# Hybrid decoder layer on one core: the residual scaled at the front, sums of squares inside the out-projection, and all top-k look-ups on VectorE

## The chip, the cores and the metric

One core of a Trainium2 chip runs the whole layer in one launch. The metric is device time in microseconds (us), the median of several executions. The engines are TensorE (PE, with its weight loads as PEld), VectorE (DVE), ScalarE (ACT), GpSimd (POOL) and SyncE (SP, which only issues transfers here). Each runs its own instructions in order; semaphores tie them together.

## The reference, cut to what matters

All arrays are float32. D is 1024, there are 1024 positions and 16 learned tokens in front of them that are dropped at the end.

```python
h = layer_norm(concat([meta, x]), ln_emb_g, ln_emb_b)
q, k, v, xr, gr = split(h @ w_in)                     # 5 x 512 columns
attn = stick_breaking_attention(q, k, v)              # 8 heads of 64
lru  = rg_lru(causal_conv(xr)) * gelu(gr)
mixed = concat([rms_norm(attn, attn_norm_g), rms_norm(lru, lru_norm_g)]) @ w_out
h = layer_norm(DEEPNORM_ALPHA * h + mixed, ln1_g, ln1_b)

# PEER: for each of 8 heads, the 16 best of 128 x 128 experts by two half keys
s1, s2 = q1 @ sub_keys[0].T, q2 @ sub_keys[1].T       # 128 scores each
v1, i1 = top_k(s1, 16);  v2, i2 = top_k(s2, 16)
sc, sel = top_k(all sums v1 + v2, 16)
idx = take(i1 * 128 + i2, sel)                        # the look-up
w = softmax(sc) * gelu(down[idx] . h)
h = layer_norm(DEEPNORM_ALPHA * h + sum(w * up[idx]), ln2_g, ln2_b)
```

## The kernel before, in words

Positions are worked in eight blocks of 128. The program is one straight list of instructions; a planner sorts each engine's list at build time by readiness and priority (earlier source lines first), and instructions issued through the handle `W` instead of `V` keep their order. A tile's memory is reused once every reader of the old tile is done, and `bufs` says how many copies a name has.

**Front (the loop over `LNB`, L278 to L302).** Nine `xt` tiles are loaded, normalised by ACT in place (L281), stored to the scratch array `xh_d` from the POOL queue (L283), transposed by PE, and split into a high and a low part `hT` (DVE, L297 and L300). Every product in the kernel is three matmuls of such parts (`mm3`, L127 to L129). The tiles of the recurrent unit, `y` first, then take over the memory of the front's pools `ga` and `lw`.

**Recurrent unit and attention (to L607).** The last of four pairs of heads (p == 3) also holds the recurrent half of the out-projection. `lru_load(j)` loads a block `hr` back from `xh_d` and POOL multiplies it by `eg` and adds `eb` (L556, L557), the embedding norm's scale and shift times ALPHA. `lru_mix` adds the projected part into `hr` on DVE (L567) and stores it to `ah_d`. On the attention path DVE does a scan (L481) and a product (L482) for each unit, PE transposes the result, and DVE or ACT copies the transposes (`aT`, L505 and L507) for the product with the values (`po`, L513).

**Out-projection (`mix_out`).** `prep(j+1)` runs one block ahead of `body(j)`: it loads the attention output into `ml`, squares it (`sq`, one buffer, L548), splits it in place into `mh` and `ml`, sums the squares on PE (`ss`, L633) and forms `rra`, the inverse root (L635). `body(j)` multiplies two halves of 512 columns and adds each, times `rra`, to the block (L645). `tail(j-1)` transposes the block before for the next stage.

**Queries and top-k (`queries`).** For each of 8 heads PE makes queries and scores, and one or two "run-ahead" products (`run_ahead`) in between; all their weights are split by DVE (`dl`, L124). DVE picks the 16 best (`topk1`, `topk_pos`). `topk_look` then builds a one-hot tile `oh` on DVE (L740) and reduces it on an engine that is passed to it:

```python
W.tensor_tensor(oh, ab.., iotb, op=is_equal)            # L740, DVE
G.tensor_tensor(oh, oh, ib.., op=mult)                  # L741
G.tensor_tensor(oh[.. 0:8], oh[.. 0:8], oh[.. 8:16])    # L742, then L743, L744: halves again
G.tensor_tensor(selo[half], oh[.., 0], oh[.., 1])       # L745
```

For heads 0 to 6 that engine is POOL, for head 7 it is DVE. From head 2 on, `hyb(1)` calls between the picks handle block 5 of the positions row by row: POOL issues an indirect gather of an expert's row (`row`, L894; at most five in flight) and DVE takes its dot product with the block (L113, `row<-row,acc`) or adds it (L922).

**Gate matrices (the loop at L1000 on).** DVE (`bt` L1016, `ae` L1021), ACT and PE build the dense gates, with more `hyb` and run-ahead work in between, and `topk_x` does the same top-k for the last two blocks with pinned instructions; its look-up is on POOL too, with one `oh` buffer (`OHX = 1`).

**Main loop.** All experts' products for five blocks on PE, and gathered rows for the other blocks on DVE.

Of the kernel before, what the change touches and what calls it, by code (L numbers as in the profile page):

```python
# [8 lines left out]
F32 = mybir.dt.float32  # L9
# [4 lines left out]
AF = mybir.ActivationFunctionType  # L14
ALU = mybir.AluOpType
# [4 lines left out]
P = 128  # L20
# [5 lines left out]
NT = S // P  # L26
NB = NT + 1
AW = 512
H = 8
# [3 lines left out]
EPS = 1e-5  # L33
# [4 lines left out]
ST = 2  # L38
# [21 lines left out]
OHX = 1  # L60
# [16 lines left out]
def layer_kernel(ctx, tc, x, meta, vecs, chan, lnc, w_in, gate_w, w_out, wq, skT, down, downT, up, out, dbg=None):  # L77
# [111 lines left out]
    with ExitStack() as c1:  # L189
# [53 lines left out]
        with ExitStack() as c2:  # L243
            ga = c2.enter_context(tc.tile_pool(name="ga", bufs=1, reuse_waits="tile"))
            lw = c2.enter_context(tc.tile_pool(name="lw", bufs=3, reuse_waits="tile"))
            tps = c2.enter_context(tc.tile_pool(name="tps", bufs=4, space=PSUM, reuse_waits="tile"))
            mv9 = ga.tile([P, NT + 1, 2], F32, name="mv9")
            ve9 = ga.tile([P, NT + 1], F32, name="ve9")
            rs9 = ga.tile([P, NT + 1], F32, name="rs9")
            nm9 = ga.tile([P, NT + 1], F32, name="nm9")  # L250
            V.memset(mv9, 1.0)
            xts = []
            for j in range(NT + 1):
                n = NM if j == 0 else P
                xt = lw.tile([P, D], F32, name="xt", bufs=NT + 1)
                SY.dma_start(xt[:n], meta if j == 0 else x[(j - 1) * P:j * P, :])
                xts.append(xt)
            convs = {i: conv_in(i) for i in range(XE)}

            def stats(j):  # L260
                n = NM if j == 0 else P
                st = small.tile([P, 2, 6], F32, name="lnst", tag="lnst")
                for i in range(2):
                    W.bn_stats(st[:n, i, :], xts[j][:n, i * 512:(i + 1) * 512])
                W.bn_aggr(mv9[:n, j], st[:n])

            for j in range(LNB[0][1]):
                stats(j)
            for bi, (j0, j1) in enumerate(LNB):
                js = slice(j0, j1)  # L270
                W.tensor_scalar(ve9[:, js], mv9[:, js, 1], EPS, None, op0=ALU.add)
                rsqrt_small(rs9[:, js], ve9[:, js], P, j1 - j0, f"ln{bi}", ga, W, (lambda: stats(j1)) if bi < 2 else None)
                W.scalar_tensor_tensor(nm9[:, js], mv9[:, js, 0], -1.0, rs9[:, js], op0=ALU.mult, op1=ALU.mult)
                if bi < 2:
                    for j in range(j1 + 1, LNB[bi + 1][1]):
                        stats(j)
            prep_slab()
            for j0, j1 in LNB:  # L278
                for j in range(j0, j1):
                    n = NM if j == 0 else P  # L280
                    A.activation(xts[j][:n], xts[j][:n], AF.Identity, bias=nm9[:n, j:j + 1], scale=rs9[:n, j:j + 1])  # L281
                    if j > 0:
                        G.dma_start(xh_d[(j - 1) * P:j * P, :], xts[j])  # L283
                c0 = 0 if j0 == 0 else NM + (j0 - 1) * P
                w = NM + (j1 - 1) * P - c0
                for c in range(KC):
                    pt = tps.tile([P, 512], F32, name="tr")
                    o = 0
                    for j in range(j0, j1):
                        n = NM if j == 0 else P  # L290
                        transpose(pt[:, o:o + n], xts[j][:n, c * P:(c + 1) * P])
                        o += n
                    tm = lw.tile([P, 3 * P], F32, name="tm")
                    A.activation(tm[:, :w], pt[:, :w], AF.Identity, bias=lc[:, 1, c:c + 1], scale=lc[:, 0, c:c + 1])
                    hi, lo = hT[0][:, c, c0:c0 + w], hT[1][:, c, c0:c0 + w]
                    if c % 2:
                        V.tensor_copy(hi, tm[:, :w])  # L297
                    else:
                        A.activation(hi, tm[:, :w], AF.Copy)
                    V.tensor_tensor(lo, tm[:, :w], hi.bitcast(F32), op=ALU.subtract)  # L300
                for xr, gen in convs.values():
                    next(gen)  # L302

        with ExitStack() as c2:
            vt = ap.tile([P, NB, AW], F32, name="vt")
# [246 lines left out]
            def lru_load(j):  # L552
                mh, ml = mixed(4, j)
                hr = wr.tile([P, D], F32, name="raw")
                SY.dma_start(hr, xh_d[j * P:(j + 1) * P, :])
                G.tensor_tensor(hr, hr, eg, op=ALU.mult)  # L556
                G.tensor_tensor(hr, hr, eb, op=ALU.add)  # L557
                return mh, ml, hr

            def lru_mix(j, mh, ml, hr):  # L560
# [13 lines left out]
            for p in range(4):  # L574
                cur = res.pop()
                gen = pair(p + 1, res) if p < 3 else iter(())
                for j in range(NT):
                    u = (p, j, *cur)
                    bes = att_a(u)
                    if prev is not None:  # L580
                        att_b(*prev)
                    prev = (u, bes)
                    next(gen, None)
                    if p == 2 and j == 6:
                        hctx.close()
                        wr = mixc.enter_context(tc.tile_pool(name="wr", bufs=2, side="right", reuse_waits="tile"))
                        wo = mixc.enter_context(tc.tile_pool(name="wo", bufs=2, side="right", reuse_waits="tile"))
                        mp = mixc.enter_context(tc.tile_pool(name="mp", bufs=1, side="right", reuse_waits="tile"))
                        mpa = mpx.enter_context(tc.tile_pool(name="mpa", bufs=1, side="right", reuse_waits="tile"))
                        eg = load_vec(mp, 0, "eg")  # L590
                        eb = load_vec(mp, 1, "eb")
                        A.activation(eg, eg, AF.Copy, scale=ALPHA)
                        A.activation(eb, eb, AF.Copy, scale=ALPHA)
                    if p == 2 and j >= 6:
                        for c in (4, 5) if j == 6 else (6, 7):
                            load_wo(c, wr, mpa)
                    if p == 2 and j == 7:
                        lnext = lru_load(0)
                    if p == 3:
                        lcur = lnext  # L600
                        if j + 1 < NT:
                            lnext = lru_load(j + 1)
                        lru_mix(j, *lcur)
                        if 2 <= j < 6:
                            load_wo(j - 2, wr, mp)
# [13 lines left out]
    def mix_out(h1, hTd, hTs):  # L619
        with mixc as c1:  # L620
# [5 lines left out]
            def prep(j):  # L626
                mh, ml, sq = first if j == 0 else mixed(0, j)
                SY.dma_start(h1[j], ah_d[j * P:(j + 1) * P, :])
                mv = wm.tile([P, 1], F32, name="mva")
                rra = wm.tile([P, 1], F32, name="rra")  # L630
                ss = sps.tile([P, 1], F32, name="ss")
                for c in range(4):
                    PE.matmul(ss, sq[:, c], ones, start=(c == 0), stop=(c == 3))  # L633
                V.tensor_scalar(mv, ss, 1.0 / AW, EPS, op0=ALU.mult, op1=ALU.add)
                rsqrt_small(rra, mv, P, 1, "ra", wm)  # L635
                return mh, ml, rra

            def body(j, mh, ml, rra):
                for hf in range(2):
                    cs = slice(hf * 512, hf * 512 + 512)  # L640
                    ps = zps.tile([P, 512], F32, name="z")
                    for c in range(4):
                        wh, wl = wch[c]
                        mm3(ps, mh[:, c], ml[:, c], wh[:, cs], wl[:, cs], c == 0, c == 3)
                    V.scalar_tensor_tensor(h1[j][:, cs], ps, rra, h1[j][:, cs], op0=ALU.mult, op1=ALU.add)  # L645
                layer_norm(h1[j], h1[j], P, None, None, None, None)

# [99 lines left out]
    def queries(hTd, hTs, zps, sps, pool, tkw, iotb, tv, sel):  # L747
# [3 lines left out]
        def second(h, vv, ii):  # L751
            cand = topk_cand(tkw, DT, vv)
            yield
            ab = topk_pos(V, tkw, DT, cand, tv[:, h])
            yield
            hs = slice(h * TOPK, (h + 1) * TOPK)
            topk_look(V, tkw, iotb, DT, ab, ii, [sel[:, half, :, hs] for half in range(2)], V if h == H - 1 else G, 2)
            yield

        def step():  # L760
# [181 lines left out]
    with ExitStack() as c1:  # L942
# [12 lines left out]
        def topk_x(h):  # L955
# [15 lines left out]
            ab = topk_pos(W, tkxw, ST, cand, tvx[:, h])  # L971
            yield
            hs = slice(h * TOPK, (h + 1) * TOPK)
            topk_look(W, tkxw, iotx, ST, ab, ii, [selx[:, half, :, hs] for half in range(2)], G, OHX)
            yield

        def index_x(h):
# [267 lines left out]
```

## Time and profile before

| | |
|---|---|
| median of 3 runs | 2960.87 us (2960.4 to 2962.03) |
| the profiled execution, its own time | 2963.82 us |
| its span in the profile | 2962.0 us, 44399 instructions |
| PE busy | 2783.2 us (94%) |
| PEld busy | 2492.6 us (84%) |
| DVE busy | 2487.0 us (84%) |
| ACT busy | 1148.1 us (39%) |
| POOL busy | 1453.4 us (49%) |
| mean granted PE clock | 0.973 |

Busy time is the time in which an engine has at least one instruction in work. Instructions of one engine overlap a little at their ends, so a sum of durations is slightly above the busy time. A granted clock of 1.00 is TensorE's upper level (2.4 GHz), 0.5 its lower (1.2 GHz); a mean in between says for what part of the stretch it was lowered.

### The profile page before, as it was taken

The page shows a single profiled execution, that of the slowest core. Times are in us where ns is not written, and L with a number is a line of the kernel's source. Part 1 is how long each engine was busy: PE and PEld are TensorE (multiplying, and loading weights), DVE is VectorE, ACT ScalarE, POOL GpSimd, SP SyncE. Part 2 cuts the span into 40 slices and gives each one's busy share as a digit, 9 for nine tenths or more (in the row PEclk, how much of TensorE's full clock was granted, in tenths as well). Part 3 has the DMA queues.
Part 4 walks back from the last instruction along what each step waited for, and adds up shares of the span by engine and source line. Part 5 has one row for each costly group of instructions (what it writes and reads, how often), then busy time and mean ns, then how long its engine had stood idle before and what let it go on. Part 6 is the DMA issues. An engine that isn't in the chain of part 4 may idle for free.

```text
span 2962.0 us, 44399 instructions
## 1 busy us (share of the span) xinstructions
PE 2783.2 (94%) x16311; PEld 2492.6 (84%) x16311; DVE 2487.0 (84%) x4610; ACT 1148.1 (39%) x2245; POOL 1453.4 (49%) x1202
## 2 busy tenths in 40 slices
PE   7999988889879989899989999999999999999997
PEld 6997766679879988889888888888888888888886
DVE  6246667768999999998769999999999999899997
ACT  6445553452212239787752223222222232222222
POOL 0003223343676655645435555556555666665653
PEclk9999988899989999999999999999999999999999
DMA  5123143413656668888789999999999999999992
GB/s 175 30 79 72 39 99 125 149 52 109 218 182 231 229 222 275 276 272 265 236 286 343 353 351 345 347 357 350 335 356 359 349 340 353 350 346 352 334 325 79
DMA packets 353946, 736.32 MB, mean 249 GB/s; under 512 B 26032, under 2 KB 164272, under 8 KB 353728
## 3 DMA queue, kind: packets, MB, share of 16 engines
q0 software_dynamic: 114304, 415.35, 39.5%
q1 hardware_dynamic: 234816, 316.03, 31.7%
q8 instruction: 128, 2.10, 0.3%
q10 hardware_dynamic: 4608, 2.10, 0.2%
q14 instruction: 90, 0.74, 0.1%
HBM read 645.24 MB, written 79.69 MB: 245 GB/s over the span
## 4 chain that ended last, share of the span: by engine, by line
PE 34%; DVE 23%; issue 17%; POOL 12%; DMA 11%; ACT 3%; SPq 0%; POOLq 0%; DVEq 0%; ACTq 0%
POOL row L894 9%; DMA row<-up,idx 6%; DVE row L113 4%; PE pp L127 3%; PE dps L127 3%; PE pp L128 3%; PE dps L129 3%; PE dps L128 3%; PE pp L129 3%; DVE dl L124 2%; DMA row<-down,idx 2%; PE g L1026 2%; PE po L513 2%; DVE h1s L1082 2%; PE z L127 2%
## 5 line engine op out<-in xcount | busy, mean ns | idle before, releaser
L127 PE MATMUL dps<-hTd,dl 128*128 128x320 f32 x2048 | 651.2, 318 | 47.0 <-DVE dl L124 40.7
L129 PE MATMUL dps<-hTd,dh 128*128 128x320 f32 x2048 | 646.6, 316 | 2.0 <-DVE hTd L124 2.0
L128 PE MATMUL dps<-hTd,dh 128*128 128x320 f32 x2048 | 647.3, 316 | 0.0
L894 POOL DMA_INDIRECT row<-down,idx x256 | 357.6, 1397 | 226.5 <-DVE act L113 188.8
L894 POOL DMA_INDIRECT row<-up,idx x256 | 343.6, 1342 | 233.9 <-DVE h1s L1082 196.3
L127 PEld LDWEIGHTS dps<-hTd,dl 128*128 128x128 f32 x2048 | 391.2, 191 | 53.0 <-DVE dl L124 32.9
L127 PE MATMUL ups<-uh,wl 128*128 128x512 f32 x1024 | 406.9, 397 | 2.6 <-DVE wl L124 2.0
L128 PE MATMUL ups<-uh,wh 128*128 128x512 f32 x1024 | 406.9, 397 | 0.0
L129 PE MATMUL ups<-ul,wh 128*128 128x512 f32 x1024 | 406.2, 397 | 0.5 <-DVE ul L124 0.5
L128 PEld LDWEIGHTS dps<-hTd,dh 128*128 128x128 f32 x2048 | 391.5, 191 | 3.0
L129 PEld LDWEIGHTS dps<-hTd,dh 128*128 128x128 f32 x2048 | 390.7, 191 | 2.3 <-DVE hTd L124 2.3
L1082 DVE SCALAR_TENSOR_TENSOR h1s<-row,gws,h1s 128x1024 f32<-128x1024 f32 x256 | 328.2, 1282 | 29.6 <-DMA row<-up,idx 27.5
L113 DVE CUSTOM_DVE_ANT_0 row<-row,h1s 128x1024 f32<-128x1024 f32 x256 | 307.1, 1221 | 36.8 <-DMA row<-down,idx 34.3
L123 ACT ACTIVATE wh<-gl 128x640 fp32r<-128x640 f32 x128 | 101.3, 792 | 606.4 <-DVE gl L1138 344.6
L894 POOL DMA_INDIRECT row<-up,idh x128 | 185.4, 1448 | 233.3 <-DVE acc L1072 84.4
L124 DVE TENSOR_TENSOR dl<-raw,dh 128x1024 fp32r<-128x1024 f32 x144 | 192.5, 1338 | 64.3 <-ACT dh L123 57.7
L129 PEld LDWEIGHTS ups<-ul,wh 128*128 128x128 f32 x1024 | 193.3, 189 | 48.3 <-DVE ul L124 1.0
L127 PEld LDWEIGHTS ups<-uh,wl 128*128 128x128 f32 x1024 | 193.2, 189 | 47.6 <-DVE wl L124 2.4
L128 PEld LDWEIGHTS ups<-uh,wh 128*128 128x128 f32 x1024 | 193.1, 189 | 44.0
L894 POOL DMA_INDIRECT row<-down,idh x128 | 162.2, 1267 | 136.2 <-DVE ach L113 23.8
L123 ACT ACTIVATE uh<-raw 128x1024 fp32r<-128x1024 f32 x128 | 133.0, 1056 | 176.5 <-PE keep L128 167.0
L113 DVE CUSTOM_DVE_ANT_0 row<-row,acc 128x1024 f32<-128x1024 f32 x128 | 176.1, 1381 | 13.0 <-DMA row<-down,idh 13.0
(583 smaller groups left out, 6194.3 us busy)
## 6 DMA issues: line engine op xcount, KB each, us to landing
raw<-downT SPq DMA_DIRECT2D x128, 512.0 KB
raw<-up SPq DMA_DIRECT2D x128, 512.0 KB
Gd<-gst SPq DMA_DIRECT2D x20, 2048.0 KB
gl<-Gd SPq DMA_DIRECT2D x128, 320.0 KB
ge_d<-ge SPq DMA_DIRECT2D x56, 320.0 KB
gex<-ge_d SPq DMA_DIRECT2D x56, 320.0 KB
wraw<-w_in SPq DMA_DIRECT2D x20, 512.0 KB
raw<-wq SPq DMA_DIRECT2D x16, 512.0 KB
```

Source lines behind the costliest of these rows:

```text
L113: return lambda *a, **k: pin(getattr(V, name)(*a, **k))
L123: A.activation(hi, src, AF.Copy)
L124: V.tensor_tensor(lo, src, hi.bitcast(F32), op=ALU.subtract)
L127: PE.matmul(o, ll, rh, start=start, stop=False, **kw)
L128: PE.matmul(o, lh, rh, start=False, stop=False, **kw)
L129: PE.matmul(o, lh, rl, start=False, stop=stop, **kw)
L513: PE.matmul(po[64 * e:64 * e + 64], vt[:m, b, p * P + 64 * e:p * P + 64 * e + 64], aTs[e][:m, b], start=(b == 0), stop=(b == nb - 1))
L894: G.indirect_dma_start(out=row, out_offset=None, in_=src, in_offset=bass.IndirectOffsetOnAxis(ap=ix, axis=0))
L1026: PE.matmul(gpt[:, q], bt[:, q], at[:, q], start=True, stop=True)
L1082: pin(V.scalar_tensor_tensor(h1s[:, j], row, gws[:, j, s:s + 1], h1s[:, j], op0=ALU.mult, op1=ALU.add))
```

## The change

The scale and shift of the residual move from the attention's last pair to the front: `eg` and `eb` are loaded there, DVE applies them to the eight `xt` tiles after the transposes, and the store to `xh_d` is issued by SP after that, from POOL no longer. In `mix_out` the four `ss` matmuls and the chain to `rra` move from `prep` into `body`, between the two halves, with a shorter chain (`rsqrt_one`: three one-operand DVE steps after the reciprocal's, where `rsqrt_small` has four), and both halves are added after the second. All look-ups take DVE.

```diff
@@ front
                     A.activation(xts[j][:n], xts[j][:n], AF.Identity, ...)
-                    if j > 0:
-                        G.dma_start(xh_d[(j - 1) * P:j * P, :], xts[j])
...
+            eg = load_vec(ga, 0, "eg")
+            eb = load_vec(ga, 1, "eb")
+            A.activation(eg, eg, AF.Copy, scale=ALPHA)
+            A.activation(eb, eb, AF.Copy, scale=ALPHA)
+            for j in range(1, NT + 1):
+                V.tensor_tensor(xts[j], xts[j], eg, op=ALU.mult)
+                V.tensor_tensor(xts[j], xts[j], eb, op=ALU.add)
+                SY.dma_start(xh_d[(j - 1) * P:j * P, :], xts[j])
@@ lru_load
                 SY.dma_start(hr, xh_d[j * P:(j + 1) * P, :])
-                G.tensor_tensor(hr, hr, eg, op=ALU.mult)
-                G.tensor_tensor(hr, hr, eb, op=ALU.add)
@@ attention, p == 2 and j == 6
-                        eg = load_vec(mp, 0, "eg")
-                        eb = load_vec(mp, 1, "eb")
-                        A.activation(eg, eg, AF.Copy, scale=ALPHA)
-                        A.activation(eb, eb, AF.Copy, scale=ALPHA)
@@ mix_out, prep
-                for c in range(4):
-                    PE.matmul(ss, sq[:, c], ones, start=(c == 0), stop=(c == 3))
-                V.tensor_scalar(mv, ss, 1.0 / AW, EPS, op0=ALU.mult, op1=ALU.add)
-                rsqrt_small(rra, mv, P, 1, "ra", wm)
-                return mh, ml, rra
+                return mh, ml, sq
@@ mix_out, body
                         mm3(ps, mh[:, c], ml[:, c], wh[:, cs], wl[:, cs], c == 0, c == 3)
+                    halves.append((cs, ps))
+                    if hf == 0:
...
+                        for c in range(4):
+                            PE.matmul(ss, sq[:, c], ones, start=(c == 0), stop=(c == 3))
+                        V.tensor_scalar(mv, ss, 1.0 / AW, EPS, op0=ALU.mult, op1=ALU.add)
+                        rsqrt_one(rra, mv, P)
+                for cs, ps in halves:
                     V.scalar_tensor_tensor(h1[j][:, cs], ps, rra, h1[j][:, cs], op0=ALU.mult, op1=ALU.add)
@@ queries
-            topk_look(V, tkw, iotb, DT, ab, ii, [...], V if h == H - 1 else G, 2)
+            topk_look(V, tkw, iotb, DT, ab, ii, [...], V, 2)
@@ topk_x
-            topk_look(W, tkxw, iotx, ST, ab, ii, [...], G, OHX)
+            topk_look(W, tkxw, iotx, ST, ab, ii, [...], W, OHX)
```

## Rows read from the trace of the kernel before

**Rows 1.** Windows: length, busy PE, PEld, DVE, ACT, POOL, granted clock, DMA.

```profile
20.00:50.00 30.00, 29.20 (x177) 26.47 (x178) 17.70 (x47) 25.64 (x45) 2.67 (x5) 1.00 0.43 153
50.00:70.00 20.00, 18.08 (x119) 16.00 (x120) 17.84 (x38) 10.83 (x17) 0.61 (x4) 1.00 0.38 109
430.00:560.00 130.00, 108.33 (x611) 80.33 (x608) 91.54 (x75) 45.37 (x118) 51.87 (x40) 0.87 0.34 111
558.00:662.00 104.00, 89.31 (x465) 76.73 (x465) 75.13 (x163) 61.97 (x131) 43.60 (x17) 0.92 0.32 106
...
690.00:1094.00 404.00, 358.50 (x2328) 355.25 (x2327) 375.51 (x1395) 90.58 (x159) 250.48 (x192) 0.95 0.61 202
...
1094.00:1508.00 414.00, 376.07 (x2637) 359.11 (x2635) 365.70 (x885) 331.37 (x824) 214.81 (x187) 0.97 0.83 263
```

**Rows 2.** Groups of DVE, 690 to 1094 us: busy, mean ns, idle before.

```profile
L113 DVE CUSTOM_DVE_ANT_0 row<-row,acc 128x1024 f32<-128x1024 f32 x96 | 133.3, 1395 | 13.0 <-DMA row<-down,idh 13.0
L124 DVE TENSOR_TENSOR dl<-raw,dh 128x1024 fp32r<-128x1024 f32 x38 | 61.5, 1624 | 13.8 <-ACT dh L123 10.9 <-ACT qt L780 2.8
...
L740 DVE TENSOR_TENSOR oh<-ab,iotb 128x1536 bf16<-128x1536 bf16 x16 | 22.8, 1424 | 0.0
```

**Rows 3.** Single tiles and lines: ns least, median, most; first and last start.

```profile
L113 DVE CUSTOM_DVE_ANT_0 row<-row,acc x128: 1196/1216/3785, 738.0 to 1244.1; 128x1024 f32<-128x1024 f32 x128
L922 DVE SCALAR_TENSOR_TENSOR acc<-row,gwh,acc x48: 1265/1278/2775, 1250.3 to 1505.1; 128x1024 f32<-128x1024 f32 x48
...
L740 DVE TENSOR_TENSOR oh<-ab,iotb x16: 937/951/3533, 698.0 to 1088.3; 128x1536 bf16<-128x1536 bf16 x16
...
L1021 DVE TENSOR_TENSOR ae<-iob,sTb x160: 397/415/1983, 1102.5 to 1502.9; 128x512 bf16<-128x512 bf16 x160
...
L548 ACT ACTIVATE sq<-ml x8: 613/626/633, 536.6 to 624.0; 128x512 f32<-128x512 f32 x8
...
L124 DVE TENSOR_TENSOR ml<-ml,mh x16: 674/685/2873, 432.1 to 626.3; 128x512 fp32r<-128x512 f32 x16
```

**Rows 4.** Window of head 7, instructions on `oh` alone: length, DVE busy.

```profile
1085.00:1094.00 9.00, 7.38 (x12) 0.88 0.61 171
```

**Rows 5.** Timeline of POOL, 813 to 820 us: start, length.

```profile
813.95 3.62 POOL L741 TENSOR_TENSOR oh<-oh,ib 128x1536 bf16<-128x1536 bf16 x1 [0.96 <-DVE oh L740]
```

**Rows 6.** Timeline of DVE, 813 to 820 us.

```profile
813.73 1.21 DVE L113 CUSTOM_DVE_ANT_0 row<-row,acc 128x1024 f32<-128x1024 f32 x1
...
814.88 3.78 DVE L113 CUSTOM_DVE_ANT_0 row<-row,acc 128x1024 f32<-128x1024 f32 x1
```

**Rows 7.** Groups of DVE, 1094 to 1508 us.

```profile
L1021 DVE TENSOR_TENSOR ae<-iob,sTb 128x512 bf16<-128x512 bf16 x160 | 76.9, 490 | 6.7 <-ACT at__10685 L1023 1.1 <-ACT at__12776 L1023 1.0 <-ACT at__13752 L1023 1.0
L922 DVE SCALAR_TENSOR_TENSOR acc<-row,gwh,acc 128x1024 f32<-128x1024 f32 x48 | 66.1, 1376 | 0.0
...
L113 DVE TENSOR_TENSOR oh<-ab,iotb 128x512 bf16<-128x512 bf16 x16 | 6.7, 421 | 15.7 <-POOL selx L745 15.7
```

**Rows 8.** Groups of DVE, 430 to 560 us (last pair of heads).

```profile
L482 DVE TENSOR_TENSOR be<-be,om 128x400 f32<-128x400 f32 x2 | 4.9, 2454 | 0.0
...
L481 DVE TENSOR_TENSOR_SCAN om<-om 128x528 f32<-128x528 f32 x2 | 4.0, 1990 | 0.8 <-ACT om L478 0.8
```

**Rows 9.** The same groups, 250 to 400 us (earlier pairs).

```profile
L481 DVE TENSOR_TENSOR_SCAN om<-om 128x528 f32<-128x528 f32 x4 | 5.0, 1254 | 1.1 <-ACT om L478 1.1
...
L482 DVE TENSOR_TENSOR be<-be,om 128x400 f32<-128x400 f32 x4 | 2.3, 573 | 0.3
```

**Rows 10.** Waits, 430 to 560 us: us in total, times, longest.

```profile
PE po L513 <- DVE aT L505: 18.5, 6, 5.1
```

**Rows 11.** Waits, 558 to 662 us.

```profile
PE ss L633 <- ACT sq L548: 7.9, 4, 3.8
```

**Rows 12.** Timeline of DVE, 25 to 57 us.

```profile
49.87 1.23 DVE L124 TENSOR_TENSOR v<-wraw,v 128x1024 fp32r<-128x1024 f32 x1
...
54.34 1.19 DVE L124 TENSOR_TENSOR v<-wraw,v 128x1024 fp32r<-128x1024 f32 x1
```

**Rows 13.** Timeline of PE, 50 to 57 us.

```profile
55.59 0.39 PE L129 MATMUL pp<-v,hT 128*128 128x256 f32 x1 [0.81 <-DVE v L124]
```

More of the change, by code (lines that the diff above doesn't have):

```diff
@@ L628, in prep, with body @@
                 SY.dma_start(h1[j], ah_d[j * P:(j + 1) * P, :])
-                mv = wm.tile([P, 1], F32, name="mva")
-                rra = wm.tile([P, 1], F32, name="rra")
-                ss = sps.tile([P, 1], F32, name="ss")
-                for c in range(4):
-                    PE.matmul(ss, sq[:, c], ones, start=(c == 0), stop=(c == 3))
-                V.tensor_scalar(mv, ss, 1.0 / AW, EPS, op0=ALU.mult, op1=ALU.add)
-                rsqrt_small(rra, mv, P, 1, "ra", wm)
-                return mh, ml, rra
-            def body(j, mh, ml, rra):
+                return mh, ml, sq
+            def body(j, mh, ml, sq):
+                halves = []
                 for hf in range(2):
@@ L644, in body @@
                         mm3(ps, mh[:, c], ml[:, c], wh[:, cs], wl[:, cs], c == 0, c == 3)
+                    halves.append((cs, ps))
+                    if hf == 0:
+                        mv = wm.tile([P, 1], F32, name="mva")
+                        rra = wm.tile([P, 1], F32, name="rra")
+                        ss = sps.tile([P, 1], F32, name="ss")
+                        for c in range(4):
[3 more added lines that the diff above has]
+                for cs, ps in halves:
                     V.scalar_tensor_tensor(h1[j][:, cs], ps, rra, h1[j][:, cs], op0=ALU.mult, op1=ALU.add)
@@ L756, in second @@
             hs = slice(h * TOPK, (h + 1) * TOPK)
-            topk_look(V, tkw, iotb, DT, ab, ii, [sel[:, half, :, hs] for half in range(2)], V if h == H - 1 else G, 2)
+            topk_look(V, tkw, iotb, DT, ab, ii, [sel[:, half, :, hs] for half in range(2)], V, 2)
             yield
@@ L973, in topk_x @@
             hs = slice(h * TOPK, (h + 1) * TOPK)
-            topk_look(W, tkxw, iotx, ST, ab, ii, [selx[:, half, :, hs] for half in range(2)], G, OHX)
+            topk_look(W, tkxw, iotx, ST, ab, ii, [selx[:, half, :, hs] for half in range(2)], W, OHX)
             yield
```

## Prediction

> **What bounds the kernel now.** I read the page's 40 slices first, to find the stages in which PE is not solid, then windows over each stage, then the groups of instructions by shape in each, and the waits and the timeline around single stalls. The main loop from 1508 us on has no edited line and only shifts; five stretches matter.
>
> In 690 to 1094 us (queries and top-k) DVE is busy 375.5 of 404 us, PE 358.5 [rows 1]. DVE sets the pace there, and of its 28.5 idle us, 13.0 are spent waiting for a gathered row [rows 2]. It is also slower than it needs to be. The dot product takes 1216 ns in the median [rows 3] but 1395 in the mean [rows 2], and the timeline says when: just before 815 us one takes 1.21 us, the next, while POOL works on `oh`, 3.78 [rows 5, 6]. The reader should see that POOL's look-up stretches DVE's two-operand instructions beside it, and holds up the gathers queued behind it on POOL, whose rows DVE then waits for.
>
> In 1094 to 1508 us DVE (365.7), PE (376.1) and ACT (331.4 of 414) are close [rows 1]; DVE waits 15.7 us for the look-up's only `oh` buffer [rows 7]. In 430 to 560 us no engine is full (PE 108.3 of 130, at a granted clock of 0.87) [rows 1]: it is a chain, and PE waits 18.5 us for `aT` [rows 10], which comes after the scan and the product on DVE. These two take 1990 and 2454 ns beside POOL's residual work, and 1254 and 573 in earlier pairs of heads, at the same sizes [rows 8, 9]. In 558 to 662 us PE is busy 89.3 of 104 us [rows 1] and waits 7.9 us for `sq` [rows 11]. In 20 to 70 us PE is busy 47.3 of 50 us [rows 1] and bounds the stage.
>
> **A, the front: +8 us (0 to +21.6).** Added on DVE: 16 two-operand instructions of 128x1024, for which the free dot of the same size gives 1.22 us [rows 3], so 19.5 us; on ACT two scalings, an estimate of 1.05 us each, since half that width takes 0.63 [rows 3], so 2.1. DVE is free 12.3 of the 30 us to 50 us, but only 2.2 of the 20 us after [rows 1]. The first blocks' tiles can be scaled in the free part once their transposes are through; I let 9 us go there. The other 10.5 come when `v` is to be split, at 49.87 and 54.34 us [rows 12]. PE already waits 0.81 us for the second of these [rows 13]; the first has about 2.5 us of slack, which leaves 8. `y` also reuses memory of these vectors, so it can't overtake them. All of it before the split is the upper bound, 19.5 + 2.1; nothing, if the order puts it in gaps, the lower. The two loads and eight stores move onto SP, eight issues leave POOL; the stores wait for DVE there, and the weight loads behind them wait too. That is inside the same bounds, since those loads need buffers that DVE frees.
>
> **B, the last pair of heads: -14 us (0 to -21.7).** Removed: 16 POOL instructions and two loads with their scalings. Ten groups of scans and products in 430 to 560 us have two instructions each beside the same size in 250 to 400 us; their means differ by 23.4 us in sum (the first and the last stand in [rows 8, 9]). PE can gain no more than its idle 21.7 us [rows 1]. I take three quarters of its 18.5 us wait for `aT` [rows 10]; what is late next is ACT's share of the same copies. If the chain is held elsewhere, nothing is gained.
>
> **D, the sums of squares: -5 us (-7.9 to +10.4).** The wait of 7.9 us goes [rows 11], and each block's chain has one DVE step less. But `sq` has one buffer: the next block's square now waits for sums taken between the halves, and its in-place split (`ml`) waits for the square. Behind the square on ACT are `tail`'s copies, behind `ml` on DVE the additions. Chain: 0.63 us for the square, 0.69 for the split, up to 2.87 beside POOL [rows 3]. Cover: the second half and eight transposes, which I put at 4 us, a little over a third of PE's 89.3/8 = 11.2 us per block [rows 1]. With an allowance of 1.8 us in ACT's queue the worst chain is 5.3 us, 1.3 over the cover; 8 x 1.3 = 10.4 is the upper bound.
>
> **E, look-ups in the queries: -11 us (-26 to +25.4).** Head 7 already looks up on DVE: 7.38 us busy on `oh`, 1.90 of it the two comparisons that DVE makes anyway [rows 4, 3], so 5.5 per head, 7 x 5.5 = 38.4 us added. Stretched time now, mean less free median [rows 2, 3]: dots 96 x 0.179 = 17.2, `dl` 38 x 0.408 = 15.5 (same size as the dot), comparisons 16 x 0.473 = 7.6, together 40.3. Nine tenths (36) should come back; gathers and the candidate sums stay on POOL. The 13.0 us for rows go. 38.4 - 36 - 13 = -10.6. If all 28.5 idle us went, -26; if no stretch came back, 38.4 - 13 = +25.4.
>
> **F, look-ups in `topk_x`: -5 us (-9 to +8.3).** 16 half look-ups with a third of the elements. The trace has none on DVE at that size: the larger costs 2.74 us per half, and a third of that is 0.91. I take 1.5, since short instructions keep a fixed part: 24 us. Coming back: `ae` 160 x 0.075 = 12.0 and `row` additions 48 x 0.098 = 4.7 [rows 7, 3]; and the wait of 15.7. 24 - 16.7 - 15.7 = -8.4; I take some half, since PE and ACT are as close to the bound. If nothing came back but the wait: +8.3.
>
> The Trainium skill (SBUF — State Buffer, "SBUF: two separate sides") says that VectorE and GpSimd share one port pair under an exclusive lock, taken for a whole instruction, and the loser waits it out. The 3.78 us dot beside the 3.62 us POOL instruction agrees with this. By that rule all 40.3 us come back, and E would be about -15.
>
> **Sum.** 8 - 14 - 5 - 11 - 5 = -27 us. The profiled execution took 2963.8 us (span 2962.0, 1.8 around it), so 2936.8 on its own scale; it stands 2.9 above the median 2960.9, and on the median's scale the forecast is 2934 us.
>
> **Rivals.**
> *Contention stays (12%).* DVE is the bound, and it gets 38.4 + 24 us more; if the stretched time is due to the gathers, which POOL keeps, only the two waits go: 62.4 - 28.7 = +33.7, with A, B, D -11 it is +23: 2984. It decides when less than 23 of the 57.0 us counted as stretched come back. For it: POOL is busy 250 of the 404 us [rows 1], and every dot needs a gather from it. Against it: the dot of 3.78 us stands under a look-up, and half of all dots are within 20 ns of the least [rows 3].
> By the Trainium skill's rule (Perfetto Trace Analysis, "Identifying the Most-Contended Engine") the engine with the highest occupancy is to be relieved first, and this change loads it; taken alone, with nothing handed back, that gives +62.4 - 11, or 3012. The rows on stretched instructions speak against it.
>
> *One of three terms fails (20%).* The last pair's gain is hidden (B 0): -13, 2948. Or the `sq` chain stalls each block (D +10.4): -11.6, 2949. Or DVE does all the scaling before the split (A +21.6): -13.4, 2947.5. For the first speaks that PE's clock there is already 0.87; for the second the single buffer; for the third that source order puts the scaling ahead of the split.
>
> *Two of them fail (12%).* About +1 to +2: 2962, no change.
>
> *All covers hold (11%).* A 0, B -21.7, D -7.9, E -26, F -9: -65, 2896.
>
> **How the numbers follow.** The forecast itself has 45%, with a range of its own of 2920 to 2945. About 0.2% (6 us) is what a measurement of this kernel can tell from no change. Faster: the 45, 18 of the 20, and the 11: 74%. Same: 10% (most of the two failures, a little of the one). Slower: the 12 and 4 of the two failures: 16%. For the range I leave out the 12% at 2984 and the outer half of the 11% at 2896, and reach over the two failures: 2905 to 2965.
>
> **What would show it.** E: dots and `dl` in the query stretch with means near 1.22 us, no wait of DVE for a `down` row after a look-up, the stretch near 393 us. F: no wait of `oh` on `selx`, the stretch near 409. B: products of 400 elements near 0.6 us, PE's wait for `aT` a few us. D: no PE wait on `sq`; a wait of `z` on `ml` instead would be its rival. A: a PE gap near 54 us, or later if the planner moves other products there. What would make it wrong: a planner that orders one of these stages anew around the moved work, long DVE runs in front of `dl`, or the front's scaling spread so that each `hT` part comes late.

## The result, and the profile after

The changed kernel takes 2921.73 us in the median of five executions (2918.79 to 2927.07), the kernel before 2960.87 in the same comparison: ratio 0.9866 [0.9848, 0.9885]. That is 39 us faster, where 27 were forecast (2934), and inside the range. The profiled executions stand at 2921.73 (span 2919.9) and 2963.82 (span 2962.0).

The time is best read by stages, each between two starts that both kernels have. The column "after" is the changed kernel. Stages: A to the first `po`; B to ACT's last copy of a `po`; C to the first `qt`; E to ACT's first copy of the queries' last `sc`; then to the first `bt`; F from there to the first matmul of `ups`; rest.

| stage, us | before | after | change | forecast |
|---|---|---|---|---|
| A front, recurrent unit | 234.3 | 249.5 | +15.2 | +8 |
| B attention | 323.8 | 286.6 | -37.2 | -14 |
| C out-projection (step D) | 102.8 | 95.7 | -7.1 | -5 |
| E queries | 395.1 | 371.9 | -23.2 | -11 |
| to the first `bt` | 45.4 | 46.3 | +0.9 | 0 |
| F gate matrices | 438.3 | 454.1 | +15.8 | -5 |
| rest | 1422.3 | 1415.8 | -6.5 | 0 |

The changes add up to the 42.1 us between the two spans. The forecast had the sign of the sum right and missed several terms, two of them badly and in opposite directions. The windows of after, with the columns of [rows 1], say where to look:

```profile
20.00:50.00 30.00, 28.71 (x173) 26.96 (x174) 22.11 (x48) 25.34 (x44) 0.00 (x0) 1.00 0.27 90
50.00:70.00 20.00, 6.45 (x31) 5.25 (x30) 20.00 (x24) 5.35 (x10) 0.00 (x0) 0.71 0.44 172
...
69.00:75.50 6.50, 6.11 (x18) 4.67 (x19) 6.29 (x10) 3.52 (x5) 0.13 (x2) 0.50 0.49 145
430.00:538.00 108.00, 101.94 (x634) 75.36 (x634) 69.97 (x80) 49.67 (x132) 12.46 (x32) 0.95 0.43 143
538.00:632.00 94.00, 85.45 (x457) 74.27 (x456) 71.46 (x155) 61.33 (x130) 42.69 (x17) 0.93 0.34 116
690.00:1042.00 352.00, 321.30 (x2123) 319.28 (x2122) 346.13 (x1347) 82.90 (x146) 133.00 (x120) 0.96 0.69 225
1042.00:1465.00 423.00, 380.11 (x2602) 365.96 (x2601) 365.76 (x971) 329.50 (x823) 152.92 (x109) 0.96 0.82 259
```

Against [rows 1]: from 50 to 70 us PE has fallen from 18.08 busy us to 6.45 under a DVE that is full; in the last pair of heads it is busy 94% of the window, at a clock of 0.95 instead of 0.87; in the queries POOL's work has halved.

**The front.** The timeline of DVE, then of PE, after:

```profile
53.86 2.35 DVE L306 TENSOR_TENSOR xt<-xt,eg 128x1024 f32<-128x1024 f32 x2
...
60.67 2.35 DVE L307 TENSOR_TENSOR xt<-xt,eb 128x1024 f32<-128x1024 f32 x2
62.94 1.56 DVE L352 TENSOR_SCALAR y<-xr,ch 128x1040 f32<-128x1040 f32 x2
...
65.70 1.22 DVE L124 TENSOR_TENSOR v<-wraw,v 128x1024 fp32r<-128x1024 f32 x1
...
68.14 1.19 DVE L124 TENSOR_TENSOR v<-wraw,v 128x1024 fp32r<-128x1024 f32 x1
```

```profile
58.90 0.58 PE L127 MATMUL pp<-v,hT 128*128 128x256 f32 x1 [4.29 <-ACT v L123]
...
69.39 0.58 PE L129 MATMUL pp<-v,hT 128*128 128x256 f32 x1 [9.26 <-DVE v L124]
69.77 0.41 PE L127 MATMUL pp<-v,hT 128*128 128x256 f32 x1
```

Eight of the 16 scalings found gaps before 53.4 us; the other eight stand in a row from 53.86 to 62.94. Behind them come `y`, which reuses their memory, and only then the split of `v`, which began at 49.87 before [rows 12]. PE's two waits are 13.55 us long where two of 1.24 in sum stood (0.43 for ACT's `v`, 0.81 for DVE's [rows 13]): 12.3 more. The rest of the 15.2 is the clock: after the waits the matmuls run at 0.50, and PE's busy time in the whole stage rose from 214.9 to 218.3 us for the same 1410 matmuls. The stores that moved to SP did not add to it. The next weight load in SP's queue,

```profile
66.98 2.94 SPq L206 DMA_DIRECT2D wraw<-w_in  x2
```

goes out when the first split of `v` ends (66.92) and its buffer comes free, as at 51.12 us before, where that split ended at 51.10.

**Queries and gate matrices.** Groups of DVE, 690 to 1042 us, then 1042 to 1465 us:

```profile
L113 DVE CUSTOM_DVE_ANT_0 row<-row,acc 128x1024 f32<-128x1024 f32 x96 | 116.4, 1221 | 0.0
L124 DVE TENSOR_TENSOR dl<-raw,dh 128x1024 fp32r<-128x1024 f32 x35 | 42.6, 1217 | 6.8 <-ACT dh L123 6.8
L745 DVE TENSOR_TENSOR oh<-oh,ib 128x1536 bf16<-128x1536 bf16 x14 | 24.5, 1752 | 0.0
...
L744 DVE TENSOR_TENSOR oh<-ab,iotb 128x1536 bf16<-128x1536 bf16 x14 | 13.3, 951 | 0.0
```

```profile
L1025 DVE TENSOR_TENSOR ae<-iob,sTb 128x512 bf16<-128x512 bf16 x160 | 65.9, 416 | 8.7 <-ACT at__10677 L1027 1.2 <-ACT at__12768 L1027 1.0 <-ACT at__13744 L1027 1.0
...
L124 DVE TENSOR_TENSOR dl<-raw,dh 128x1024 fp32r<-128x1024 f32 x27 | 33.1, 1226 | 44.0 <-ACT dh L123 44.0
...
L113 DVE TENSOR_TENSOR oh<-ab,iotb 128x512 bf16<-128x512 bf16 x16 | 6.6, 415 | 0.0
```

In the queries the stretch of [rows 2] is gone (means from 1395 to 1221 ns, 1624 to 1217, 1424 to 951, beside the medians of [rows 3]), and so are the 13.0 us of waits for rows. In the gate stage the wait of `oh` for `selx` of [rows 7] is gone too, and `ae` is back at its free median [rows 3]; but DVE now waits 44.0 us for `dh`. The same group before, 1094 to 1508 us:

```profile
L124 DVE TENSOR_TENSOR dl<-raw,dh 128x1024 fp32r<-128x1024 f32 x27 | 32.9, 1217 | 22.3 <-ACT dh L123 22.3
```

The `dl` splits of the run-ahead products by time, in the stage's first part (windows on `dl` alone; behind the length stand DVE's busy time on it and the count), first before, then after:

```profile
1112.00:1137.00 25.00, 2.41 (x2) 1.00 0.88 275
1137.00:1234.00 97.00, 4.83 (x4) 1.00 0.89 282
1234.00:1287.00 53.00, 4.88 (x4) 0.90 0.83 265
```

```profile
1060.00:1085.00 25.00, 2.37 (x2) 1.00 0.91 272
1085.00:1182.00 97.00, 0.05 (x1) 0.93 0.89 279
1182.00:1235.00 53.00, 10.02 (x8) 0.94 0.58 195
```

and all engines of after in nearly the same stretches:

```profile
1050.00:1115.00 65.00, 60.61 (x442) 57.66 (x440) 63.06 (x178) 59.50 (x152) 26.91 (x18) 1.00 0.90 281
1115.00:1180.00 65.00, 44.72 (x258) 41.12 (x259) 63.75 (x192) 55.25 (x147) 29.28 (x22) 0.91 0.86 267
1180.00:1245.00 65.00, 63.40 (x434) 62.70 (x433) 37.50 (x87) 34.51 (x81) 10.32 (x9) 0.94 0.57 191
```

For almost 100 us no product is prepared: DVE is full with gates and picks, PE is idle for 20 of 65 us; then eight are prepared at once, PE is solid, and DVE and ACT wait for it. Before, they came one or two at a time in this part of the stage, mostly 15 to 25 us apart.

### The profile page after: what moved, and what is told of

It is laid out like the page before. It is cut to its first block, busy times and chain, and to the rows that moved or that the text cites. A ratio compares the mean times of both kernels' runs of the same rounds, so it can differ in the third digit from the quotient of the medians.

```text
span 2919.9 us, 44345 instructions
## 1 busy us (share of the span) xinstructions
PE 2771.6 (95%) x16311; PEld 2490.4 (85%) x16311; DVE 2468.0 (85%) x4768; ACT 1146.0 (39%) x2245; POOL 1224.4 (42%) x1028
## 3 DMA queue, kind: packets, MB, share of 16 engines
q0 software_dynamic: 113152, 411.16, 39.7%
## 4 chain that ended last, share of the span: by engine, by line
PE 50%; DVE 15%; issue 6%; POOL 3%; ACT 3%; DMA 2%; SPq 0%; POOLq 0%; DVEq 0%; ACTq 0%
PE dps L127 6%; PE dps L129 6%; PE dps L128 6%; PE ups L127 6%; PE ups L128 6%; PE ups L129 6%; PE g L1030 5%; DVE row L113 4%; POOL row L898 3%; DVE dl L124 2%; PE keep L129 2%; PE keep L128 2%; PE keep L127 2%; ACT gst L1031 1%; DMA row<-down,idx 1%
## 5 line engine op out<-in xcount | busy, mean ns | idle before, releaser
L127 PEld LDWEIGHTS dps<-hTd,dl 128*128 128x128 f32 x2048 | 388.9, 190 | 38.4 <-DVE dl L124 20.2
L1086 DVE SCALAR_TENSOR_TENSOR h1s<-row,gws,h1s 128x1024 f32<-128x1024 f32 x256 | 328.3, 1282 | 16.1 <-DMA row<-up,idx 14.0
L898 POOL DMA_INDIRECT row<-up,idh x128 | 189.7, 1482 | 305.5 <-DVE acc L1076 95.8
L124 DVE TENSOR_TENSOR dl<-raw,dh 128x1024 fp32r<-128x1024 f32 x144 | 179.7, 1248 | 80.5 <-ACT dh L123 80.0
L1176 DVE TENSOR_TENSOR acc<-acc,ups 128x512 f32<-128x512 f32 x252 | 171.9, 682 | 16.8 <-PE ups L129 16.6
```

The lines of the kernel that those rows point to most:

```text
L124: V.tensor_tensor(lo, src, hi.bitcast(F32), op=ALU.subtract)
L127: PE.matmul(o, ll, rh, start=start, stop=False, **kw)
L898: G.indirect_dma_start(out=row, out_offset=None, in_=src, in_offset=bass.IndirectOffsetOnAxis(ap=ix, axis=0))
L1086: pin(V.scalar_tensor_tensor(h1s[:, j], row, gws[:, j, s:s + 1], h1s[:, j], op0=ALU.mult, op1=ALU.add))
L1176: V.tensor_tensor(h1[j][:, hsl], h1[j][:, hsl], ps, op=ALU.add)
```

## The experiments

All times are medians of four executions; ratios are to the kernel before, run on the same chip. Stages in us, as in the table above. The first four kernels ran together, so did the next four, and the last four; the kernel before took 2960.5, 2962.64 and 2961.59 in these three sets.

| kernel | time | ratio | A | B | C | E | F |
|---|---|---|---|---|---|---|---|
| look-up of `topk_x` on POOL | 2903.39 | 0.9817 [0.9792, 0.9842] | 248.8 | 286.4 | 91.2 | 370.5 | 438.7 |
| run-ahead spread | 2865.02 | 0.9684 [0.9668, 0.97] | 247.0 | 287.8 | 94.7 | 369.5 | 395.0 |
| scaled late on DVE | 2903.65 | 0.9817 [0.9796, 0.9837] | 234.8 | 286.4 | 95.8 | 369.4 | 447.9 |
| not scaled | 2904.86 | 0.9815 [0.9797, 0.9833] | 234.2 | 287.8 | 94.8 | 369.4 | 451.1 |
| look-ups of the queries on POOL | 2934.75 | 0.9919 [0.989, 0.9949] | 247.5 | 287.4 | 89.8 | 396.0 | 451.5 |
| POOL at work beside | 3006.53 | 1.0141 [1.011, 1.0172] | 247.6 | 287.8 | 94.7 | 435.9 | 453.6 |
| before, not scaled | 2932.75 | 0.9902 [0.9879, 0.9925] | 234.5 | 292.4 | 103.7 | 395.0 | 438.8 |
| sums back in `prep` | 2929.03 | 0.989 [0.9866, 0.9913] | 247.6 | 287.3 | 101.9 | 369.5 | 447.5 |
| spread, scaled late | 2850.79 | 0.9627 [0.9603, 0.9651] | 234.6 | 286.7 | 95.8 | 369.4 | 395.0 |
| spread, `topk_x` on POOL | 2880.32 | 0.9722 [0.9693, 0.975] | 248.6 | 288.1 | 94.6 | 369.5 | 417.5 |
| before, spread | 2935.6 | 0.9913 [0.9885, 0.9941] | 233.3 | 320.0 | 102.8 | 394.9 | 414.8 |
| spread, late, second call behind the picks | 2867.27 | 0.9683 [0.9658, 0.9707] | 234.2 | 286.6 | 94.4 | 388.2 | 398.4 |

A stage is read from one profiled execution. How far to trust it shows in kernels that share its lines. F is 447.5 to 454.1 us in the six that have it as after, though DVE's instructions stand there in the same order in all six. C is 89.8 to 95.8 in the ten with step D, 101.9 to 103.7 in the four without. A is 247.0 to 249.5 with the scaling at the front, 233.3 to 234.8 without. A difference of 6 us between two kernels in C or F says little by itself.

**Step F undone.**

```diff
-            topk_look(W, tkxw, iotx, ST, ab, ii, [...], W, OHX)
+            topk_look(W, tkxw, iotx, ST, ab, ii, [...], G, OHX)
```

> The changed kernel with the look-up of topk_x alone back on POOL. Theory: the move of this look-up is what costs 15.8 us between the first bt and the first ups (438.3 us before, 454.1 after), because DVE's waits on selx were the slots in which the planner put the run-ahead dl splits; some 6.5 us of it is given back in the main loop. So the stretch goes back to about 438 us, dl stands in it about every 20 us again, and the time is 9 to 12 us below the changed kernel: 2911. Rival: the queries' look-ups shifted the planner's order, and topk_x on DVE itself saves the 5 us of the prediction: then the stretch stays near 454 or grows, and the time is 2922 to 2927.

F fell from 454.1 to 438.7, before's length, and the time by 18. The move of this look-up alone accounts for the longer stage; by the range above it cost 9 to 16 us. The surplus came mostly from stage C, 4.5 us shorter although PE, DVE and ACT run the same instructions there in the same order; why it was shorter is not known.

**Run-ahead spread.** The same 31 calls, written between the groups:

```diff
                     hyb(HGW)
                     topk_turn(DF * P // 8)
+                    while ra_done < (t8 // 8 + 1) * RAG[j] // (P // 8):
+                        run_ahead()
+                        ra_done += 1
...
-            for c in range(RAG[j]):
-                run_ahead()
```

> The changed kernel with the run-ahead calls of the gate stage written between the groups of eight columns instead of behind each block of 16 groups. Theory: the 15.8 us are lost because the run-ahead products stand in clumps (no dl from 1084 to 1183 us, then eight in 50 us), so that first DVE and ACT are full with PE idle and then PE alone is full; spread out, PE's repeated 1.43 us waits for at go and the stretch from the first bt to the first ups falls from 454 to 438 us or less: 2900 to 2912. Rival: what costs is the added 24 us of DVE work itself, which no order removes: the stretch stays at 450 to 455 and the time at 2918 to 2924.

F fell by 59 us, to 395.0, far below the kernel before, and the time to 2865, below the theory's 2900 to 2912: it named the cause and underrated it. Windows on `dl` as above, then the whole stage on all engines, of this kernel and, last, of after:

```profile
1060.00:1085.00 25.00, 2.41 (x2) 1.00 0.96 305
1085.00:1182.00 97.00, 7.32 (x6) 1.00 0.94 303
1182.00:1235.00 53.00, 6.05 (x5) 1.00 0.88 284
```

```profile
1046.00:1441.00 395.00, 380.39 (x2785) 369.52 (x2783) 371.02 (x970) 337.05 (x835) 150.35 (x108) 1.00 0.90 291
```

```profile
1050.00:1504.00 454.00, 408.12 (x2780) 393.72 (x2779) 374.57 (x972) 340.16 (x837) 152.60 (x108) 0.96 0.82 261
```

DVE does the same work in both. PE's idle time fell from 45.9 to 14.6 us, and its busy time for the same products by 27.7: the idle time had been paid nearly twice. The clock, 1.00 instead of 0.96, accounts for part of that. A mean of 0.96 over 454 us is some 36 us at the lower level, half the speed, which lengthens the busy time by 18 us at most; the other ten are not explained.

**Where the residual is scaled.** Late on DVE, and not at all (the second kernel leaves the scale and shift out, so the residual goes in as it is):

```diff
@@ lru_load (late on DVE; the front stores as before the change)
                 SY.dma_start(hr, xh_d[j * P:(j + 1) * P, :])
+                V.tensor_tensor(hr, hr, eg, op=ALU.mult)
+                V.tensor_tensor(hr, hr, eb, op=ALU.add)
@@ p == 2 and j == 7, behind load_wo
+                        eg = load_vec(mp, 0, "eg")
...
@@ front (both kernels)
-            for j in range(1, NT + 1):
-                V.tensor_tensor(xts[j], xts[j], eg, op=ALU.mult)
...
```

> The changed kernel with the residual scaled on DVE when the last pair of heads loads it, not at the front; eg and eb are loaded behind the w_out loads of that pair. Theory: the front's 15.2 us come back (eight scalings in a row delay y and the split of v), and DVE, busy 62 of 98 us in the last pair, hides most of 19.5 us there: 0 to 5 us lost, so 2907 to 2912. Rival: the scalings fall between scan, product and copies of the attention's chain, PE waits for aT again and its clock falls: up to 20 us lost, 2920 to 2927.

> The changed kernel with the residual's scale and shift left out altogether (work left out; the stores go out from POOL behind the normalisation as before the change). It gives the floor for step A. Theory: all of the front's cost is the 16 DVE scalings, packed in front of y and v: the first po at 234 us again and the time 15 us lower, 2906 to 2908. Rival: part of the cost is the move of the stores and loads into SP's queue or another order of the projections on PE: less than 10 us come back.

Stage A is back at 234.8 and 234.2. Both kernels also move the loads and the stores back, so they do not part these from the scaling; the SP row above does so for the stores. Their times are 1 to 3 us below the two theories. Late on DVE costs nothing that can be seen: B is 286.4 us with the scalings on DVE, 287.8 without any. The window of the last pair in the kernel that scales late:

```profile
413.00:521.00 108.00, 101.49 (x632) 74.24 (x632) 89.64 (x98) 53.57 (x139) 13.37 (x33) 0.95 0.48 155
```

DVE carries 19.7 us more than after in as long a window (89.64 for 69.97), and PE is busy as long. So the front was the wrong place for the scaling, and what was wrong with the old place was the engine, and the order of two loads (below).

**Step E undone, and POOL busy for nothing.**

```diff
@@ look-ups of the queries on POOL
-            topk_look(V, ..., V, 2)
+            topk_look(V, ..., V if h == H - 1 else G, 2)
@@ POOL at work beside (per half, on a scratch tile)
+                for k in range(0, DT, 2):
+                    GP.tensor_tensor(dm, iotb[:, k:k + 2], ib[:, half, k:k + 2]..., op=ALU.mult)
+                    for m in (8, 4, 2, 1):
+                        GP.tensor_tensor(dm[:, :, 0:m], dm[:, :, 0:m], dm[:, :, m:2 * m], op=ALU.add)
```

> The changed kernel with the look-ups of heads 0 to 6 back on POOL (step E undone). Theory: the step is worth what the landmarks say, 23 us from the first qt to the last sc (395.1 us before, 371.9 after): all of the 40.9 us of stretch and the 13 us of row waits come back as a cost, and the look-ups' own time is saved: 2942 to 2947. Rival: the step itself is worth the predicted 11 us and the other 12 came from the earlier stages' shift: 2930 to 2935.

> The changed kernel, in which POOL does look-up work beside DVE's on a scratch tile that nobody reads (added work: per half, three products of 512 elements and the halvings, as many elements as the look-up has). Theory: POOL's own instructions stretch DVE's two-operand instructions: dots and dl in the query stretch go back from means of 1220 and 1217 ns towards 1.4 and 1.6 us, the gathers queue behind them, and the time rises by 25 to 45 us: 2947 to 2967. Rival: the stretch came from the look-up's data passing from DVE to POOL and back, or from the gathers, not from POOL being at work: the means stay within 30 ns of 1.22 us and the time is at most 2928.

With the look-ups back on POOL stage E is 396.0 us, close to before's 395.1 and 24.1 above after, so the step is worth what the stage showed. The whole time rose by 13 only, into the rival's range, since other stages came out shorter (C by 5.9 us, F by 2.6, the rest by 2.9), again with nothing edited there.

POOL's idle work brought more than the theory said: 85 us. The dots take 1.28 us in the mean and `dl` 1.34, less than the theory had and more than the rival allows. The stretch came back, 37 us of DVE time in all between the first `qt` and the first `bt` (sums of durations by form, this kernel less after), but 11 of it on dots and `dl` and the rest on the look-ups and the picks' small steps. The other part is waiting: each gather stands on POOL behind more instructions. The first row of DVE's waits, 630 to 1133 us, then its timeline and POOL's around one stretched dot:

```profile
DVE row L113 <- DMA row<-down,idh: 41.4, 8, 9.4
```

```profile
798.08 1.21 DVE L113 CUSTOM_DVE_ANT_0 row<-row,acc 128x1024 f32<-128x1024 f32 x1
...
799.23 2.06 DVE L113 CUSTOM_DVE_ANT_0 row<-row,acc 128x1024 f32<-128x1024 f32 x1
```

```profile
798.17 2.03 POOL L748 TENSOR_TENSOR dm<-iotb,ib 128x512 bf16<-128x512 bf16 x1
```

The rival (data passing between the engines, or the gathers) falls: nobody reads this work, and it stretches DVE; and in after, where the gathers are still POOL's, the dots are free.

**The kernel before without POOL's scalings.**

```diff
-                G.tensor_tensor(hr, hr, eg, op=ALU.mult)
-                G.tensor_tensor(hr, hr, eb, op=ALU.add)
```

> The kernel before with POOL's 16 scalings in the last pair of heads left out (work left out: the residual goes in without its scale and shift; the loads of eg and eb and ACT's two scalings stay). Theory: the 37 us that the attention got shorter are 30 of the last pair (PE's idle time and a clock that falls with it, both from POOL's scalings) and 7 of the loads, which hold up the w_out loads and ACT before it: so 28 to 31 us come back here, first po to last po goes from 323.8 to about 294, and the 8.1 us wait of PE for om near 411 us stays: 2930 to 2933. Rival: the loads and ACT's scalings are the larger part, and POOL's instructions cost at most the 14 us that the prediction put: 2945 to 2950.

B fell by 31.4 to 292.4 us, and the time to 2932.75, as the theory said (this kernel too leaves the residual unscaled). The other 5.8 of the step go with the loads: in PE's waits of the kernel before, 400 to 440 us, there stands a wait (first fence) that this kernel keeps (second fence, 400 to 527 us) and after has no longer. The third has the window of the last pair, before and in this kernel.

```profile
PE z L473 <- ACT om L478: 8.6, 3, 8.1
```

```profile
PE z L473 <- ACT om L478: 8.7, 3, 8.2
PE po L513 <- DVE aT L505: 2.2, 4, 1.0
```

```profile
432.00:558.00 126.00, 104.33 (x586) 77.23 (x585) 89.38 (x73) 43.89 (x116) 51.87 (x40) 0.88 0.34 114
432.00:527.00 95.00, 92.33 (x588) 68.32 (x588) 60.42 (x73) 43.79 (x117) 6.04 (x24) 1.00 0.41 140
```

The chain: `eg` and `eb` were issued on SP ahead of the two `w_out` loads, these arrived later, ACT waited for them (2.60 and 2.75 us) in front of the copies that `z` needed. It is their order that costs, not the loads: the kernel that scales late on DVE loads both behind `w_out` and has this left of the wait, 400 to 521 us:

```profile
PE z L473 <- ACT om L478: 2.7, 5, 0.9
```

In the last pair PE's 18.5 us for `aT` [rows 10] are down to 2.2, and the clock is 1.00.

**Step D undone.** The `ss` block goes back to `prep`, and each half is added as it is done, as in the kernel before.

> The changed kernel with the sums of squares back in the preparing step of the out-projection and the first half added at once (step D undone). Theory: PE waits for sq again, about 7 us: 2927 to 2930. Rival: the 7 us of this stage came from the quieter attention before it: 2920 to 2923.

C rose by 6.2 us to 101.9, and the time by 7.3, as the theory said. The wait of [rows 11] is back (first fence, PE's waits, 538 to 637 us); after has in its place a short one for `ml` (second, 538 to 632):

```profile
PE ss L633 <- ACT sq L554: 7.9, 4, 3.7
```

```profile
PE z L127 <- DVE ml L124: 2.1, 1, 2.1
```

(The profiled execution, 2917.87, is 11 us under the kernel's other three, so the stage, not the profiled time, is compared.)

**Both edits, and step F priced without the clumps.** Edits as above, combined.

> The changed kernel with both edits: run-ahead calls spread over the gate stage, and the residual scaled on DVE in the last pair of heads. Theory: the two lie in different stages, so the gains add: 2865 less 18, 2843 to 2852. Rival: something later (the main loop's own rows, or weights not yet loaded) absorbs the second gain: above 2856.

> The changed kernel with run-ahead spread over the gate stage and the look-up of topk_x back on POOL. It prices step F by itself, once the order is no longer in its way. Theory: there the look-up on DVE is worth what the prediction put, so without it the stage from the first bt to the first ups is 3 to 9 us longer than the 395.0 us with it: 2867 to 2875. Rival: the added DVE work costs more than the stretch and the waits it removes in any order: the stage is shorter than 393 us and the time below 2862.

> The kernel before with run-ahead calls spread over the gate stage, nothing else changed. Theory: the order with the calls behind each block was already costing there, only less, since DVE's waits for selx let some dl in; the stage falls from 438 us to 400 to 415: 2923 to 2940. Rival: before, the dl splits already stood every 20 us, so the order has nothing to gain and the loss was the change's alone: 2955 to 2963.

The two edits add, as the first theory said: 2850.79, the fastest of all, 71 us below after. With the calls spread, the look-up of `topk_x` on DVE is worth 22.5 us in its stage (417.5 to 395.0) and 15.3 in the time (the profiled execution without it, 2888.88, is the longest of its four, so the stage may flatter it). The kernel before gains 23.5 us in that stage from the spreading alone (438.3 to 414.8): the order was costing there already, as the third theory said. The second put what the look-up is worth too low (3 to 9 us).

**One order too many.**

```diff
-                for c in range(RAQ.get(hh, 0)):
+                if hh in RAQ:
                     run_ahead()
...
                 topk1(V, tkw, sbs, DT, vv[:, half], ii[:, half], lambda: hyb(1))
+                for c in range(1, RAQ.get(hh, 0)):
+                    run_ahead()
```

> As the kernel with both edits, and in the queries the second run-ahead call of each half is written behind the picks instead of in front of them. Theory: PE's waits for dl in that stage (30 us in the changed kernel, the longest 13.3) are clumps too and shrink: 4 to 12 us below the kernel with both edits. Rival: DVE sets the pace there (346 of 352 us busy), so the order of its work does nothing: within 3 us.

Neither: stage E became 18.8 us longer, with DVE waiting 27.6 us for `dh` in place of 16.1. The place of a call in the source lengthened this stage by 19 us, as it shortened F by 59; why this place is worse was not followed further.

## Why the prediction was right in sum and wrong in two terms

That the sum came out near is partly luck. Against their forecasts A and F, with the stretch before F, were worse by 28.9 us, and B, D, E and the rest better by 44.0; these errors cancel to 15. B and F lie outside the bounds that the prediction gave them.

**A, +8, measured +15.2.** The mechanism and the place were right (a gap near 54 us, the split of `v` late, `y` unable to overtake). "I let 9 us go there" was nearly right (eight scalings), and the 8 us left for the late split came as put: PE's wait for it went from 0.81 to 9.26. What the term left out is ACT's cast of `v`, which came later too (55.33 us for 48.79, now behind copies of `xr` that wait 3.48 us for PE) and added 3.9, and the half clock after both waits.

**B, -14, measured -37.2.** The step that failed is the bound: "PE can gain no more than its idle 21.7 us". PE's idle time fell by 19 (21.7 to 2.7 in the kernel before without scalings), and its busy time by 12 more for the same matmuls (104.3 to 92.3), because the clock rose from 0.88 to 1.00. And the two loads with their scalings were costed at nothing; their place ahead of `w_out` held 5.8 us.

**D, -5, measured -7.1** (6.2 when undone). The wait for `sq` went as stated. The rival showed, small: PE waits 2.1 us for `ml` once; the cover held.

**E, -11, measured -23.2** (24.1 when undone). "Nine tenths (36) should come back": all of it did: count times fall of the mean over the stage is 16.6 on dots, 15.5 on `dl`, 7.6 on comparisons, 39.7 together. The stage on all engines, before and after:

```profile
661.00:1056.00 395.00, 354.36 (x2315) 351.35 (x2314) 356.42 (x1360) 86.85 (x157) 236.60 (x181) 0.96 0.58 193
632.00:1004.00 372.00, 347.96 (x2310) 346.18 (x2310) 351.56 (x1426) 86.96 (x158) 122.31 (x113) 0.97 0.63 205
```

DVE's busy time fell by 4.9 us where 2.4 more was put (38.4 - 36): the look-ups added 35.8 us of it, and all its other work fell by 40.7. Its idle time fell by 18.1, not 13.0: the waits of `dl` for ACT shrank by 6.5 as well. Those two account for the difference.

The Trainium skill (SBUF — State Buffer, "SBUF: two separate sides") let all the stretch come back, because VectorE and GpSimd exclude each other for a whole instruction. The 39.7 us and the stretched dots agree with it. By the Trainium skill's other rule that was weighed (Perfetto Trace Analysis, "Identifying the Most-Contended Engine": the engine with the highest occupancy is to be optimized first), read as the prediction read it, loading that engine should have cost time; here, in stage E, its busy time fell by 4.9 us when it took the work over.

**F, -5, measured +15.8 in its stage, against which 6.5 fell off later.** Each size was right: 24.5 us of look-ups (24 put), 16.6 of stretch returned (16.7 put), the 15.7 us wait gone. The step that failed is that a removed wait is a gain. The wait held back the picks, whose order is pinned, and around it the planner had put the `dl` of run-ahead products, whose calls stand behind each block in the source: in the kernel before one follows within 11 us on seven of the eight waits. Without the wait gates and picks filled DVE for 100 us, then the products came in a clump: DVE's wait for `dh` doubled. That the order is what costs is shown by moving the calls alone; that the removed wait is what changed the order is an inference, since the planner's choices are not on record. Undoing F gave the stage back; spreading the calls turned the same step into a gain of 22.5. The prediction named "a planner that orders one of these stages anew" among what would make it wrong, but gave it no price.

The rest behind the first `ups` (1415.8 us) lies between 1412.9 and 1422.3 in all these kernels, though nothing is edited there. What moves it was not tested, and the 6.5 us are no effect of a step that I can name.

## What to carry to other kernels

Before counting a removed wait as a gain, ask what the scheduler put into it: on an engine with a fixed order an idle slot may be the only place where another engine's work gets prepared, and the remedy is to write that work there. Idle time of TensorE was paid here as a wait and again as a lowered clock; a bound by idle time alone was too low. And if a helper engine stretches the busiest one, give that one the work where it already has room (here the last pair), not where it is full (the front).

## What the runs showed of the hardware

A dot on DVE that starts while POOL works on a tensor-tensor instruction mostly ends a fixed time after it. Before, the dot of [rows 6] starts at 814.88 and POOL's instruction of [rows 5] ends at 817.57; the dot ends at 818.66, 1.09 us later. Beside the idle work POOL's instruction ends at 800.20 and the dot at 801.29, again 1.09 us later, though they overlapped by 2.69 us in one case and 0.97 in the other. Of the 128 dots of [rows 3], all 32 that took more than 1.24 us began within such an instruction and ended 1.08 to 1.09 us after it. Six more began within one and kept their 1.2 us; there POOL ended last, 0.1 to 2.6 us after the dot. So short POOL instructions stretch one dot less (2.07 us at most, 3.78 before), though beside the idle work other steps of DVE were stretched as well.

In the front the granted clock was 0.62 in a stretch of after in which PE was busy 1.23 of 14 us (55 to 69 us), and 0.50 in the 6.5 us after it, although PE was busy 6.11 of them; from 75 us on it was 1.00.
